# A new order for the last output projection, the router and the expert selection of an encoder layer

## The chip, the cores and the metric

One core of a Trainium2 chip runs one launch of the kernel. The metric is the device time of that launch in microseconds (us). The kernel before takes 1476.27 us, the median of three runs (1474.61, 1476.27 and 1476.34).

## What is computed

One encoder layer on 512 tokens with 1024 features, all in float32. After attention, four tiles of 128 tokens go through an output projection, a norm with a residual, a second norm, and a router that picks 4 of 32 experts for each token:

```python
mix = jnp.concatenate([o_diff, o_nat], axis=-1) @ w_out[l]
x = x + gt1 * rms_norm(mix, g_post_mix[l])
h2 = rms_norm(x, g_pre_ffn[l]) * (1.0 + sc2) + sh2
logits = (h2 @ w_router + b_router)          # 512 x 32
top_val, top_idx = lax.top_k(logits, TOP_K)  # 4 of 32
gates = softmax(top_val)
# each expert: y = swiglu_clamped(rows @ w1[e] + b1[e]) @ w2[e] + b2[e]
f = sum of gates * y over the chosen experts
x = x + gt2 * rms_norm(f, g_post_ffn[l])
```

Each expert's weights are 12 MB in float32, so the 32 experts bring 384 MB through the DMA engines.

## The kernel before

**Stages.** The kernel first does the modulation, the input projection and the two attentions. Then comes the stage in which the change lies, written out by hand for four token tiles (0 to 3), and after it 32 expert units, each of which takes 12 weight pieces of 1 MB and multiplies them with the rows of its tokens. Unit 0 has two row tiles of 32 slots, unit 1 has three.

**The order is the program's.** The stage is inside `manual_schedule`, so each engine gets its instructions in the order in which the code is written. Engines run beside each other and wait for one another by semaphores, but nothing on one engine overtakes what stands ahead of it there.

**The helpers of the stage**, with their engines and lines:

- `project_out(t, n)`: half n of the output projection of tile t, 24 matmuls of 128x512 on PE (L271 to L273), reading the split weights `wh` and `wl` and the split operands `mh` and `ml`.
- `gated(t, n)`: a square with a sum on ACT (L1066) and, on DVE, the product of the projection with a gain (L1067); the latter waits for the former.
- `mix_norm(t)` and `norm(t)`: ten tiny DVE operations each (L99 to L107), an inverse square root. `beside(...)` deals out the steps of several such generators in turn.
- `residual_in(t)`: on DVE twice the residual (L1077) and the product that gives `u` (L1079), on ACT two squares (L1080).
- `router_turn(t)`: 8 transposes of `u` on PE (L1112) and two copies `hT` on ACT (L1113).
- `router(t, tag)`: the router's products on PE (L1120, 8 calls, 16 records in the trace), which need `hT`.
- `write_h2(t)`: scales `u` on ACT (L1097), adds the shift `s2` on POOL (L1098) and writes the tile to DRAM by a DMA that POOL issues (L1102). For tile 3 the arithmetic is on DVE instead (L1101, two operations).
- `route(t)`: four DVE operations that pick the top 4 from the logits (L1132 to L1139).
- `place(t)`: small products of the choices on PE (L1147), which count the tokens ahead of each, then a DVE operation on that count (L1149) and one that makes a one-hot table `oh0` (L1151).
- `first_rows(t)`: the rows of tile t for the two experts of units 0 and 1, gathered on PE by that table into the PSUM tile `x0` (L1158, 16 matmul records).

After `first_rows(3)`, DVE subtracts one from `first` (L1258), transposes `x0` into `xt0` (L1259), and unit 0 begins on PE with L1535. On POOL the product of the last gain `gf` (L1027) follows the DMA of tile 3.

**The weight ring.** The pieces go through 14 slots of 1 MB, 4 in `rawa` and 10 in `rawb`. `feed.load()` (L143) puts the DMA of the next piece on SP's queue. The four slots of `rawa` are filled while the output weights are used up. `rawb` lies where the output weights and their operands were: `right.close()` gives that space back once the last projection is through, and then

```python
        right.close()
        rings.append(ctx.enter_context(tc.tile_pool(name="rawb", bufs=RING_B, side="right", reuse_waits="tile")))
        for _ in range(RING_B - 2):
            feed.load()
```

asks for eight pieces and, at the end of the stage, two more. From then on each of the 12 steps of a unit frees a slot and asks for one piece.

Of the kernel before, what the change touches and what calls it, by code (L numbers as in the profile page):

```python
# [59 lines left out]
def encoder_layer(ctx: ExitStack, tc: tile.TileContext, x, c, w_ada, b_ada, g_pre_mix, g_post_mix,  # L60
# [33 lines left out]
    def rstd_steps(pool, st):  # L94

        ss = st[:, 0:1]
        w = pool.tile([P, 3], F32, name="rq")
        y, h, q = w[:, 0:1], w[:, 1:2], w[:, 2:3]
        nc.vector.tensor_add(ss, ss, st[:, 1:2])  # L99
        nc.vector.tensor_scalar(ss, ss, 1.0 / D, EPS, ALU.mult, ALU.add)  # L100
        yield
        nc.vector.tensor_scalar(y.bitcast(I32), ss.bitcast(I32), -0.5, 1597463007.0, ALU.mult, ALU.add)
        nc.vector.tensor_scalar(h, ss, -0.5, None, ALU.mult)
        yield
        for i in range(3):
            nc.vector.scalar_tensor_tensor(out=q, in0=y, scalar=h, in1=y, op0=ALU.mult, op1=ALU.mult)
            nc.vector.scalar_tensor_tensor(out=ss if i == 2 else y, in0=q, scalar=1.5, in1=y, op0=ALU.add, op1=ALU.mult)  # L107
            yield
# [150 lines left out]
    def project_out(t, n=None, ks=range(KT)):  # L259
        if n is None:  # L260
            for n in range(2):
                project_out(t, n)
            return
        ns = halves[n]
        if ks[0] == 0:
            mixes.setdefault(t, []).append(pp.tile([P, 512], F32, tag=("mm", "S", "O", "mm")[t], name="mix"))
        mix = mixes[t][n]
        for k in ks:
            wh, wl = wo[k // 2]
            mh, ml = ops[t, k // 4]  # L270
            nc.tensor.matmul(mix, mh[:, k % 4, :], wh[:, k % 2, ns], start=(k == 0), stop=False)  # L271
            nc.tensor.matmul(mix, ml[:, k % 4, :], wh[:, k % 2, ns], start=False, stop=False)
            nc.tensor.matmul(mix, mh[:, k % 4, :], wl[:, k % 2, ns], start=False, stop=(k == KT - 1))  # L273
# [727 lines left out]
    with ExitStack() as m:  # L1001
# [27 lines left out]
        def residual(t):  # L1029
            res[t] = mo.tile([P, D], F32, name="res", bufs=2)  # L1030
            nc.sync.dma_start(res[t], xr[t])
# [28 lines left out]
        def gated(t, n):  # L1060

            if n == 0:
                sts[t] = o2.tile([P, 4], F32, name="st", bufs=4)
                us[t] = o2.tile([P, D], F32, name="u", bufs=4)
            ns, mix = halves[n], mixes[t][n]
            nc.scalar.activation(us[t][:, ns], mix, AF.Square, accum_out=sts[t][:, n:n + 1])  # L1066
            nc.vector.tensor_tensor(out=x1[:, t, ns], in0=mix, in1=gp[:, ns], op=ALU.mult)  # L1067

        def mix_norm(t):
            return rstd_steps(o2, sts[t][:, 0:2])  # L1070

        def residual_in(t):

            st = sts[t]
            u = us[t]
            for n, ns in enumerate(halves):
                nc.vector.scalar_tensor_tensor(out=x1[:, t, ns], in0=x1[:, t, ns], scalar=st[:, 0:1], in1=res[t][:, ns],  # L1077
                                               op0=ALU.mult, op1=ALU.add)
                nc.vector.tensor_mul(u[:, ns], x1[:, t, ns], a2[:, ns])  # L1079
                nc.scalar.activation(res[t][:, ns], x1[:, t, ns], AF.Square, accum_out=st[:, 2 + n:3 + n])  # L1080

        def norm(t):
            return rstd_steps(o2, sts[t][:, 2:4])

        def beside(*steps):

            steps = list(steps)
            while steps:
                for s in list(steps):
                    if next(s, steps) is steps:  # L1090
                        steps.remove(s)

        def write_h2(t):

            u, r2 = us[t], sts[t][:, 2:3]
            if t < NT - 1:
                nc.scalar.activation(u, u, AF.Copy, scale=r2)  # L1097
                nc.gpsimd.tensor_tensor(out=u, in0=u, in1=s2, op=ALU.add)  # L1098
            else:
                for ns in halves:  # L1100
                    nc.vector.scalar_tensor_tensor(out=u[:, ns], in0=u[:, ns], scalar=r2, in1=s2[:, ns], op0=ALU.mult, op1=ALU.add)  # L1101
            nc.gpsimd.dma_start(rows_of[0][t * P:(t + 1) * P, :], u)  # L1102

        def router_turn(t):

            hTs[t] = []
            for q in range(2):
                tp = pp.tile([P, 4, P], F32, tag="T", name="tp")
                hT = o2.tile([P, 4, P], F32, name="hT", bufs=4)
                for j in range(4):  # L1110
                    k = q * 4 + j
                    nc.tensor.transpose(tp[:, j, :], us[t][:, k * P:(k + 1) * P], ident)  # L1112
                nc.scalar.activation(hT, tp, AF.Copy)  # L1113
                hTs[t].append(hT)

        def router(t, tag):

            lg = lgs[t] = pp.tile([P, 512], F32, tag=tag, name="lg")[:, :NE]
            for k in range(KT):
                nc.tensor.matmul(lg, hTs[t][k // 4][:, k % 4, :], wr[:, k, :], start=(k == 0), stop=(k == KT - 1))  # L1120
# [8 lines left out]
        def route(t):  # L1129

            lo = lo4[:, t, :NE]
            nc.vector.scalar_tensor_tensor(out=lo, in0=lgs.pop(t), scalar=sts[t][:, 2:3], in1=br, op0=ALU.mult, op1=ALU.add)  # L1132
            yield

            nc.vector.max(top8[:, t, :], lo4[:, t, :])
            yield
            nc.vector.match_replace(rest[:, t, :], top8[:, t, :], lo4[:, t, :], -3.0e38)
            yield
            nc.vector.tensor_tensor(out=packed[:, t, 0, :], in0=rest[:, t, :NE], in1=lo, op=ALU.is_lt)  # L1139
            yield  # L1140

        def place(t):


            ps = pp.tile([P, 4, P], F32, tag="T", name="ps")[:, 0, :STATIC]
            for u in range(t + 1):
                nc.tensor.matmul(ps, tri if u == t else allone, packed[:, u, 0, :STATIC], start=(u == 0), stop=(u == t))  # L1147
            at = first[:, t, :]
            nc.vector.scalar_tensor_tensor(out=at, in0=ps, scalar=1.0, in1=packed[:, t, 0, :STATIC], op0=ALU.add, op1=ALU.mult)  # L1149
            yield  # L1150
            nc.vector.tensor_scalar(oh0[:, t, :], slot1, at[:, 0:1], None, ALU.is_equal)  # L1151
            yield

        def first_rows(t):

            for q in range(2):
                for c in range(4):
                    nc.tensor.matmul(x0[c * T:(c + 1) * T, q * SMALL:(q + 1) * SMALL], oh0[:, t, q * T:(q + 1) * T],  # L1158
                                     us[t][:, c * SMALL:(c + 1) * SMALL], start=(t + q == 0), stop=(t == NT - 1),
                                     skip_group_check=True)  # L1160
# [58 lines left out]
        residual_in(1)  # L1219
        beside(norm(1))  # L1220
        residual(3)
        router(0, "S")
        project_out(3, 0)
        for n in range(2):
            gated(2, n)
        beside(mix_norm(2))
        router_turn(1)
        write_h2(1)
        residual_in(2)
        beside(norm(2), route(0))  # L1230
        gated(3, 0)
        project_out(3, 1)
        right.close()
        rings.append(ctx.enter_context(tc.tile_pool(name="rawb", bufs=RING_B, side="right", reuse_waits="tile")))
        for _ in range(RING_B - 2):
            feed.load()
        gated(3, 1)
        router(1, "S")
        router_turn(2)
        write_h2(2)  # L1240
        beside(mix_norm(3), place(0), route(1))
        x0 = pp.tile([P, 512], F32, tag="S", name="x0")
        first_rows(0)
        router(2, "O")
        residual_in(3)
        beside(place(1), route(2))
        router_turn(3)
        first_rows(1)
        beside(norm(3), place(2))
        router(3, "O")  # L1250
        first_rows(2)
        beside(route(3))
        write_h2(3)
        beside(place(3))
        first_rows(3)
# [9 lines left out]
    with ExitStack() as m:  # L1265
# [477 lines left out]
        with tc.If(n_over > 0):  # L1743
            with tc.For_i(0, n_over, 1) as v:
                place = nc.gpsimd.value_load(over_i[0:1, bass.ds(v, 1)], min_val=0, max_val=NE - 1)
# [76 lines left out]
```

## Time and profile before

| what | value |
|---|---|
| median of three runs | 1476.27 us (1474.61 to 1476.34) |
| profiled execution, its own time | 1475.74 us |
| its span on the core | 1474.2 us |
| mean granted TensorE clock | 0.934 of full |
| PE busy (matmul) | 1285.8 us, 87% of the span |
| DVE, ACT and POOL busy | 577.6, 275.1 and 309.9 us |
| moved by DMA | 487.38 MB, mean 331 GB/s |

The page gives busy time by engine, the span in 40 slices, DMA queues and the costliest groups of instructions. Times in the timeline count from the start of the span. A busy PE is modelled, since matmuls overlap; the clock column says which share of full speed the engine was granted: 1.00 is 2.4 GHz, 0.50 is 1.2 GHz.

### The profile page before, as it was taken

The numbers are of one execution on the slowest core, as the hardware profiler recorded it, in microseconds if no ns is written. First come the engines' busy times: TensorE is split into PE (matmuls) and PEld (weight loads), VectorE is DVE, ScalarE is ACT, GpSimd is POOL, SyncE is SP. The second block draws the span as 40 slices with busy tenths as digits, with TensorE's granted clock in tenths as the row PEclk, the third lists the DMA queues.
The fourth block names the chain that finished last, engine by engine and source line by source line (L and its number), as shares of the span: only waits on it lengthen the run. The fifth ranks groups of instructions, "written<-read, shape, count | busy, mean of one in ns | idle before, by whom it ended". The sixth has DMA issues, their size and how long they took to land. (4 is left out here: it accounts for less than half of the span.)

```text
span 1474.2 us, 41218 instructions
## 1 busy us (share of the span) xinstructions
PE 1285.8 (87%) x18034; PEld 796.7 (54%) x18034; DVE 577.6 (39%) x1527; ACT 275.1 (19%) x680; POOL 309.9 (21%) x337
## 2 busy tenths in 40 slices
PE   6999899789889979777779999998999998989562
PEld 4876777677445535433346555554656553545221
DVE  4778664657543323222232333332333322223114
ACT  3355343533201100001000110010101101011011
POOL 5103121223112211112120112223212221211103
PEclk7999999889699999999999999999999997979765
DMA  8746344364999999999999699999999999999992
GB/s 272 248 157 237 129 158 142 99 221 146 396 351 403 400 397 406 400 405 401 400 400 383 211 383 398 398 400 398 409 398 397 400 395 396 403 393 407 395 401 90
DMA packets 144009, 487.38 MB, mean 331 GB/s; under 512 B 15448, under 2 KB 44508, under 8 KB 127440
## 3 DMA queue, kind: packets, MB, share of 16 engines
q1 hardware_dynamic: 125136, 457.30, 79.8%
q0 software_dynamic: 18624, 27.39, 7.3%
q8 instruction: 142, 2.33, 0.6%
q14 instruction: 43, 0.35, 0.1%
q10 hardware_dynamic: 64, 0.02, 0.0%
HBM read 471.86 MB, written 21.09 MB: 334 GB/s over the span
## 5 line engine op out<-in xcount | busy, mean ns | idle before, releaser
L1535 PE MATMUL acc<-raw,xT 128*32 128x256 f32 x9984 | 574.7, 385 | 76.3 <-DMA raw<-in_w_dram 71.1
L1535 PEld LDWEIGHTS acc<-raw,xT 128*32 128x32 f32 x9984 | 316.7, 111 | 319.0 <-DMA raw<-in_w_dram 106.8
L1535 PE MATMUL acc<-raw,gT 128*32 128x256 f32 x5120 | 311.3, 395 | 33.9 <-DMA raw<-in_w_dram 32.1
L1476 DVE TENSOR_TENSOR acc<-acc,xt 128x512 f32<-128x512 f32 (+1 forms) x140 | 83.5, 601 | 618.7 <-PE acc L1535 608.3
L1535 PEld LDWEIGHTS acc<-raw,gT 128*32 128x32 f32 x5120 | 165.1, 113 | 163.0 <-DMA raw<-in_w_dram 38.9
L1504 POOL DMA_INDIRECT f_d<-y,ri x79 | 125.3, 1586 | 495.4 <-issue 174.1
L1456 POOL DMA_INDIRECT gx<-h_d,ri x78 | 81.3, 1043 | 329.7 <-DVE gt L1451 245.4
L1486 ACT ACTIVATE g<-acc 128x256 f32<-128x256 f32 (+1 forms) x96 | 33.4, 348 | 535.8 <-DVE acc L1476 535.8
L1500 ACT ACTIVATE y<-acc,gt 128x256 f32<-128x256 f32 x79 | 33.0, 471 | 208.8 <-DVE acc L1476 157.5
L1493 DVE STREAM_TRANSPOSE gT<-g 128x256 f32<-128x256 f32 (+1 forms) x96 | 55.8, 581 | 3.3
L1487 DVE TENSOR_SCALAR lin<-acc 128x256 f32<-128x256 f32 (+1 forms) x96 | 36.5, 380 | 41.6 <-ACT g L1486 41.6
L728 ACT ACTIVATE s<-s,mx 128x512 f32<-128x512 f32 (+2 forms) x64 | 40.6, 636 | 50.7 <-DVE mx L726 50.7
L1465 DVE STREAM_TRANSPOSE xT<-gx 128x512 f32<-128x512 f32 (+3 forms) x33 | 41.6, 1260 | 3.6 <-DMA gx<-h_d,ri 3.6
L305 PE MATMUL ps<-hTh,wh 128*128 128x512 f32 x96 | 40.0, 416 | 1.2 <-ACT wh L334 1.2
L306 PE MATMUL ps<-hTh,wl 128*128 128x512 f32 x96 | 38.3, 399 | 1.2 <-DVE wl L340 1.2
L307 PE MATMUL ps<-hTl,wh 128*128 128x512 f32 x96 | 38.3, 399 | 0.0
L1523 ACT ACTIVATE xt<-ps 128x512 f32<-128x512 f32 (+1 forms) x62 | 27.0, 489 | 58.6 <-PE ps L1522 58.6
L1488 DVE SCALAR_TENSOR_TENSOR g<-g,lin 128x256 f32<-128x256 f32 (+1 forms) x96 | 36.6, 381 | 3.3
L726 DVE CUSTOM_DVE_ANT_0 s<-S,tab 128x512 f32<-128x512 f32 (+2 forms) x64 | 35.1, 586 | 7.0 <-PE S L757 6.9
L834 POOL TENSOR_TENSOR tab<-mask,rb 128x256 f32<-128x256 f32 (+1 forms) x24 | 21.9, 937 | 53.9 <-DVE mx L726 33.4
L1522 PE MATMUL ps<-bias,sl 128*128 128x256 f32 (+1 forms) x128 | 32.7, 379 | 0.0
L1522 PEld LDWEIGHTS ps<-bias,sl 128*128 128x128 f32 x128 | 22.8, 199 | 17.5 <-issue 14.0
(388 smaller groups left out, 1399.9 us busy)
## 6 DMA issues: line engine op xcount, KB each, us to landing
raw<-in_w_dram SPq DMA_DIRECT2D x384, 1024.0 KB
raw<-in_w_ada_dram SPq DMA_DIRECT2D x24, 1024.0 KB
raw<-in_w_in_dram SPq DMA_DIRECT2D x9, 1024.0 KB
rpb_q<-rpb_d SPq DMA_DIRECT2D x8, 512.0 KB
raw<-in_w_out_dram SPq DMA_DIRECT2D x4, 1024.0 KB
raw<-in_w_in_dram SPq DMA_DIRECT2D x12, 256.0 KB
xin<-in_x_dram SPq DMA_DIRECT2D x8, 256.0 KB
rb<-rpb_q POOLq DMA_DIRECT2D x8, 256.0 KB, 2.9
```

Source lines behind the costliest of these rows:

```text
L305: nc.tensor.matmul(ps, ah, bh, start=(k == 0), stop=False)
L306: nc.tensor.matmul(ps, al, bh, start=False, stop=False)
L307: nc.tensor.matmul(ps, ah, bl, start=False, stop=(k == n - 1))
L728: nc.scalar.activation(s, s, AF.Exp, bias=mx, scale=-1.0, accum_out=sums)
L1456: nc.gpsimd.indirect_dma_start(self.gx[:, t * SMALL:(t + 1) * SMALL], None, h2_d, self.quarter_rows(t), bounds_check=4 * L - 1, oob_is_err ...
L1465: nc.vector.transpose(xT[:, :self.n], self.gx[:, :self.n * SMALL].rearrange("p (t i k) -> p t k i", i=T, k=KT))
L1476: nc.vector.tensor_tensor(out=acc, in0=acc, in1=v, op=ALU.add)
L1488: nc.vector.scalar_tensor_tensor(out=g, in0=g, scalar=LIMIT_GLU, in1=lin, op0=ALU.min, op1=ALU.mult)
L1493: nc.vector.transpose(self.gT[:, half, ts[0]:ts[-1] + 1], g.rearrange("p (t i b) -> p t b i", i=T, b=4))
L1504: nc.gpsimd.indirect_dma_start(f_d, self.quarter_rows(t), self.y[:, t], None, bounds_check=4 * L - 1, oob_is_err=False, compute_op=ALU.add)
L1522: nc.tensor.matmul(ps, self.sl, bias[:, part, o:o + n], start=(part == 0), stop=(part == 1))
L1535: nc.tensor.matmul(acc[(c0 + c) * T:(c0 + c + 1) * T, :], b.stationary(third, k, t), w[:, c * SMALL:(c + 1) * SMALL], start=(k == 0 and t ...
```

## The change

`router(0)` and, of tile 1, `router_turn` and `write_h2` move from between the last projections to behind them. `route(0)`, `place` and `first_rows` of tiles 0 to 2 move later: `residual_in(3)` and `router_turn(3)` now come ahead of all `place` and `first_rows`, and `router(3)` ahead of all `first_rows` but the first. No operation is added or removed.

```diff
         residual(3)
-        router(0, "S")
         project_out(3, 0)
         for n in range(2):
             gated(2, n)
         beside(mix_norm(2))
-        router_turn(1)
-        write_h2(1)
         residual_in(2)
-        beside(norm(2), route(0))
+        beside(norm(2))
         gated(3, 0)
         project_out(3, 1)
         right.close()
         rings.append(ctx.enter_context(tc.tile_pool(name="rawb", bufs=RING_B, side="right", reuse_waits="tile")))
         for _ in range(RING_B - 2):
             feed.load()
+        router(0, "S")
+        router_turn(1)
+        write_h2(1)
         gated(3, 1)
         router(1, "S")
         router_turn(2)
         write_h2(2)
-        beside(mix_norm(3), place(0), route(1))
+        beside(mix_norm(3), route(0), route(1))
+        router(2, "O")
+        residual_in(3)
+        router_turn(3)
+        beside(norm(3), place(0), route(2))
         x0 = pp.tile([P, 512], F32, tag="S", name="x0")
         first_rows(0)
-        router(2, "O")
-        residual_in(3)
-        beside(place(1), route(2))
-        router_turn(3)
+        router(3, "O")
+        beside(place(1), route(3))
         first_rows(1)
-        beside(norm(3), place(2))
-        router(3, "O")
+        beside(place(2))
         first_rows(2)
-        beside(route(3))
         write_h2(3)
         beside(place(3))
         first_rows(3)
```

On PE, around the second last half of the projection (`wh`, `wl` are its weights, `mh`, `ml` its operands), the router's products go:

```order
 L272 MATMUL mix<-wh_3050,ml 128x512
 L273 MATMUL mix<-wl_3051,mh 128x512
-L1120 MATMUL lg<-wr,hT 128x32 x8
 L271 MATMUL mix<-wh_2882,mh 128x512
 L272 MATMUL mix<-wh_2882,ml 128x512
```

The same happens to the eight transposes of tile 1 between the last two halves, so 48 projection matmuls now follow each other on PE.

On ACT, from the squares of tile 2's projection on (`x_70` is the residual stream, `u` the tile before and after scaling):

```order
 L1066 ACTIVATE u,st<-mix 128x512 x2
+L1080 ACTIVATE res,st<-x_70 128x512 x2
+L1066 ACTIVATE u,st<-mix 128x512
 L1113 ACTIVATE hT<-tp 128x512 x2
 L1097 ACTIVATE u<-u,st 128x1024
-L1080 ACTIVATE res,st<-x_70 128x512 x2
-L1066 ACTIVATE u,st<-mix 128x512 x2
+L1066 ACTIVATE u,st<-mix 128x512
 L1113 ACTIVATE hT<-tp 128x512 x2
 L1097 ACTIVATE u<-u,st 128x1024
```

The copies and the scaling of tile 1 now stand behind the first and ahead of the second of the two squares of tile 3's projection.

On PE, the end of the stage before, from the transposes of tile 3 to unit 0 (the instructions of `place`, L1147, are left out here):

```order
L1112 MATMUL tp<-ident,u 128x128 x8
L1158 MATMUL x_3750<-u,oh_3449 32x256 x8
...
L1120 MATMUL lg<-wr,hT 128x32 x8
L1158 MATMUL x_3750<-u,oh_3449 32x256 x8
...
L1158 MATMUL x_3750<-u,oh_3449 32x256 x8
L1535 MATMUL acc<-raw,xt_3231 32x256 x16
```

and in the changed kernel:

```order
L1112 MATMUL tp<-ident,u 128x128 x8
L1147 LDWEIGHTS tri
L1147 MATMUL ps<-packed,tri 128x2
L1158 MATMUL x_3794<-u,oh_3449 32x256 x8
L1120 MATMUL lg<-wr,hT 128x32 x8
...
L1158 MATMUL x_3794<-u,oh_3449 32x256 x8
...
L1158 MATMUL x_3794<-u,oh_3449 32x256 x8
...
L1158 MATMUL x_3794<-u,oh_3449 32x256 x8
L1535 MATMUL acc<-raw,xt_3231 32x256 x16
```

Behind the transposes of tile 3 three `first_rows` stood before, of which one ahead of the last router products and two behind; now four stand there, three of them behind, each behind a `place`. The order on POOL and on SP is the same in both kernels.

## Rows read from the trace of the kernel before

**Rows 1.** The page, part 2: 40 slices of 36.9 us, busy tenths of DMA.

```profile
DMA  8746344364999999999999699999999999999992
```

**Rows 2.** SP's timeline: start, us, loads of 1 MB pieces.

```profile
360.41 1062.37 SPq L143 DMA_DIRECT2D raw<-in_w_dram  x380
...
387.51 0.37 SPq L143 DMA_DIRECT2D raw<-in_w_dram  x1
```

**Rows 3.** By stretch: PE, PEld, DVE, ACT, POOL busy, granted clock, DMA share, GB/s.

```profile
368.70:388.50 19.80, 16.39 (x114) 9.29 (x115) 11.88 (x38) 2.55 (x6) 3.44 (x6) 0.50 1.01 407
...
421.00:422.00 1.00, 1.00 (x14) 0.41 (x10) 0.00 (x0) 0.00 (x0) 0.70 (x2) 0.50 0.41 148
```

**Rows 4.** PE's timeline: start, us, instruction, in brackets idle time before and releaser.

```profile
346.61 1.86 PE L1120 MATMUL lg<-wr,hT 128*128 128x32 f32 x16
348.31 0.48 PE L271 MATMUL mix<-wh,mh 128*128 128x512 f32 x1
...
353.89 1.04 PE L1112 MATMUL tp<-ident,u 128*128 128x128 f32 x8
354.68 0.48 PE L271 MATMUL mix<-wh,mh 128*128 128x512 f32 x1
...
360.22 1.86 PE L1120 MATMUL lg<-wr,hT 128*128 128x32 f32 x16
```

**Rows 5.** ACT's timeline: tile 1's copies and scaling, later tile 3's second square.

```profile
354.52 1.09 ACT L1113 ACTIVATE hT<-tp 128x512 f32<-128x512 f32 x2 [3.90 <-PE tp L1112]
355.49 1.15 ACT L1097 ACTIVATE u<-u,st 128x1024 f32<-128x1024 f32 x1
356.54 0.63 ACT L1080 ACTIVATE res<-x 128x512 f32<-128x512 f32 x1
...
360.42 0.60 ACT L1066 ACTIVATE u<-mix 128x512 f32<-128x512 f32 x1 [1.97 <-PE mix L273]
```

**Rows 6.** POOL's timeline: shifts of tiles 1 and 2, a write's issue, the gain `gf`.

```profile
356.74 2.93 POOL L1098 TENSOR_TENSOR u<-u,s 128x1024 f32<-128x1024 f32 x1 [10.36 <-ACT u L1097]
...
364.86 2.35 POOL L1098 TENSOR_TENSOR u<-u,s 128x1024 f32<-128x1024 f32 x1 [4.33 <-ACT u L1097]
367.50 0.57 POOL L1102 DMA_DIRECT2D h_d<-u  x1 [0.30 <-POOL u L1098]
...
380.73 2.37 POOL L1027 TENSOR_TENSOR gf<-gf,gv 128x1024 f32<-128x1024 f32 x1
```

**Rows 7.** DVE's timeline: ten steps of a norm (first, last), and tile 3's path.

```profile
337.90 0.15 DVE L99 TENSOR_TENSOR st<-st 128x1 f32<-128x1 f32 x1
...
339.68 0.16 DVE L107 SCALAR_TENSOR_TENSOR st<-rq 128x1 f32<-128x1 f32 x1
...
364.92 2.30 DVE L106 SCALAR_TENSOR_TENSOR rq<-rq 128x1 f32<-128x1 f32 x1
...
367.90 0.75 DVE L1077 SCALAR_TENSOR_TENSOR x<-x,st,res 128x512 f32<-128x512 f32 x1
...
370.07 0.69 DVE L1079 TENSOR_TENSOR u<-x,a 128x512 f32<-128x512 f32 x1
...
380.30 2.94 DVE L1258 TENSOR_SCALAR first<-first 128x8 f32<-128x8 f32 x1
```

**Rows 8.** PE's timeline from the transposes of tile 3's second half to unit 0.

```profile
370.89 1.11 PE L1112 MATMUL tp<-ident,u 128*128 128x128 f32 x4 [0.28 <-DVE first L1149]
...
373.91 3.60 PE L1120 MATMUL lg<-wr,hT 128*128 128x32 f32 x16
377.44 1.94 PE L1158 MATMUL x<-u,oh 128*32 128x256 f32 x16
379.31 0.24 PE L1147 MATMUL ps<-packed,allone 128*128 128x2 bf16 x3
...
380.32 1.93 PE L1158 MATMUL x<-u,oh 128*32 128x256 f32 x16 [0.75 <-DVE oh L1151]
383.81 3.64 PE L1535 MATMUL acc<-raw,xt 128*32 128x256 f32 x32 [1.55 <-DVE xt L1259]
```

## The prediction, made before the changed kernel ran

> **What bounds the kernel now.** I began with the page's 40 slices [rows 1]: DMA is busy at nine tenths or more in 28 of the 29 slices from 369 us to the last but one, so the last three quarters of the span are the stream of expert weights. SP's timeline dates it [rows 2]: 380 loads of 1 MB from 360.41 on, 1062 us for 380 MB, with little left beside it. That makes an earlier first load look like pure gain. Two more rows speak against it. The eleventh new load goes out only at 387.51 [rows 2], because the 14 slots are full until unit 0, which begins at 383.81 [rows 8], has finished its first step of 3.64 us. And at 421 us DMA falls to 0.41 of its capacity while PE works without a pause [rows 3]: the loads have caught up and wait for slots. So until about 425 us the experts are paced by when unit 0 starts and by what PE does then, not by the stream. What moves unit 0's start moves the rest of the kernel by as much; what moves the first load alone is given back in that wait.
>
> The question is thus the path to 383.81. I read it backwards on PE [rows 8], then on DVE and POOL [rows 6, 7]: last product of tile 3 on DVE (start 370.07, 0.69 long, so ready at 370.76), transposes, router, rows of the last tiles, unit 0. It takes 13.05 us from 370.76, at a granted clock of 0.50 throughout [rows 3], 1.2 GHz.
>
> **What the change does to the first load.** The router's products of tile 0 (346.61 to 348.31, 1.70 us) and the transposes of tile 1 (353.89 to 354.68, 0.79 us) leave PE's way before the last projection [rows 4]. Its end moves from 360.22 to 357.73, and the loads, which wait for it, start 2.5 us earlier. By the argument above this is worth nothing unless unit 0 starts earlier too. SP's own order is unchanged, so no load is queued behind a new wait. The DMA that writes tile 1 goes out some 5 us later; nobody reads it before the gathers that follow unit 0's start, so I cost it at nothing.
>
> **What it does to tile 3's path.** Tile 1's work now lies behind the last projection, in the stretch where only tile 3 is waited for.
>
> - PE: 357.73 + 1.70 + 0.79 gives 360.22 for the end of the transposes of tile 1; they start at 359.43, and ACT's copies follow 0.63 us behind their start [rows 4, 5], at 360.06.
> - ACT: the copies hold it 0.97 us, the scaling 1.05 [rows 5]. Behind these now stands the second square of tile 3, at 360.06 + 2.02 = 362.08 where it was at 360.42 [rows 5]: 1.7 us later, although its projection is done 2.5 us earlier.
> - POOL: the shift of tile 1 starts 1.25 us after the scaling does [rows 5, 6], at 361.03 + 1.25 = 362.28, and lasts 2.35 us [rows 6] to 364.63. The issue of its write ends 0.86 us later (364.86 + 2.35 = 367.21 to 368.07 [rows 6]), so the shift of tile 2 runs from about 365.5 to 367.9.
> - DVE: the long rows show that a tiny operation on 128x1 takes 2.30 us where it meets such a shift, 364.92 to 367.22 against POOL's 364.86 to 367.21 [rows 6, 7]. Before, tile 3's norm met one of the two shifts, tile 2's. Now it meets both: it cannot start before 364.63, does 0.9 us of work until the shift of tile 2 begins, and goes on at 367.9. The ten steps of the norm take 1.94 us alone (337.90 to 339.84 [rows 7]); for the eight steps of two `route` between them I add 0.8, an estimate, for they fill waits between dependent steps. Of 2.74 us 0.9 are done, so it ends at 369.74. `residual_in(3)` takes 2.86 us (367.90 to 370.76 [rows 7]): ready at 372.6 instead of 370.76, **+1.8 us**.
>
> **What it does to the way from there to unit 0.** Before, the rows of tiles 0 and 1 were gathered ahead of the router of tile 3, one of them while PE had nothing better to do. Now all four gathers stand behind the transposes of tile 3, each behind a `place` that PE must wait for. At the low clock of the stretch, by rows 8:
>
> - 0.13 to the transposes (370.76 to 370.89) and 1.11 for them;
> - four gathers of 1.87 (377.44 to 379.31), 7.48;
> - the router's products 3.53 (373.91 to 377.44);
> - four times a `place` with its two DVE operations, 1.01 each (379.31 to 380.32), 4.04;
> - from the last gather's end (380.32 + 1.87 = 382.19) to unit 0 1.62, of which some 0.7 was lost before, since L1258 was held until POOL had finished `gf` (380.30 + 2.94 = 383.24 against 380.73 + 2.37 = 383.10 [rows 6, 7]). Now `write_h2(3)` sits on DVE during the third gather, and `gf` is through by then: 0.9.
>
> The sum is 17.2 us against 13.05, **+4.1 us**. Unit 0 starts at 372.6 + 17.2 = 389.8, **5.9 us** later than 383.81 (1.8 and 4.1).
>
> By then the earlier loads have been waiting with full slots: the ten are in by about 388.5 (2.5 us ahead of before), and the eleventh goes out at 389.8 + 3.7 = 393.5 instead of 387.51. So 5.9 us pass to the end in full. Against the profiled execution's own 1475.74 us that gives 1481.6; the median of the runs is 0.5 above that execution, so for the median **1482.2 us**. A measurement can tell about 0.2%, 3 us; the forecast is twice that.
>
> **Bounds of what the trace doesn't show.** The clock of the tail is at one end 0.50, as taken, at the other 1.00. I take 0.50: PE now stands still from about 365 (357.73, three routers, two tiles' transposes and short waits for copies) to 371, and in the stretch from 368.7 to 388.5 work of the same kind kept it busy for 16.39 of 19.80 us without bringing the clock back [rows 3]. The meeting of DVE with the shifts costs between nothing (3.6 us less than above: 1.2 of the first, 2.4 of the second) and what I took; I take the upper end, because the shift before did block DVE for its whole length [rows 6, 7]. A `place` costs at least the 0.24 of its PE rows and at most 1.01 [rows 8]; I take 1.01, as its three links are in series.
>
> **The rivals.**
>
> *The clock comes back before unit 0, or never leaves* (not slower). If PE ran at full speed over the tail, the PE pieces above, 1.11 + 7.48 + 3.53 = 12.1 us, would halve: 6.1 less. Unit 0's own slow start from 383.81 to 388.5 would also shrink by 2.35 [rows 3, 8]. 5.9 - 6.1 - 2.35 = -2.5: 1473.7. It decides at about 371: the clock must be 1.00 when the transposes of tile 3 run. For it: 7.5 us of unbroken work up to 365. Against it: the pause after it. Chance 0.06.
>
> *It comes back in the middle of the tail*, after the second gather: two gathers at half, 1.9, and the 2.35 of unit 0, 4.2 less: +1.7, 1478.0. PE is busier there than before. Against it: from 374 to 388.5 it was about as busy before and stayed at 0.50. Chance 0.12.
>
> *The shifts miss tile 3's norm*, because POOL comes later or DVE holds it off: 3.6 less, +2.3, 1478.6. For it: the order of two engines within tenths of a microsecond decides. Against it: either shift lies ahead of the norm's end by more than a microsecond. Chance 0.08.
>
> *`gf` holds the last one-hot.* In the new order `gf` on POOL starts about 0.1 us ahead of L1151 of tile 3 on DVE (an estimate: behind the start of the third gather L1151 comes by its 1.87 and half of a `place`, 2.37; `gf` by two operations of 0.69 like L1079 and the 0.30 and 0.57 of the write's issue, 2.25 [rows 6 to 8]). If L1151 waits as L1258 did [rows 7], the last gather starts some 2.2 us later: +8.1, 1484.4. The Trainium skill, "SBUF — State Buffer", Who interferes with whom, says that a VectorE operation with a single SBUF input also takes the port it shares with GpSimd when it is of the kinds that can run in a two-port mode, and names `tensor_scalar` among them, which L1151 is. The trace agrees for L1258, 2.94 us long; no run here yet shows L1151 beside a POOL operation that reads SBUF. Against it: 0.1 us decides. Chance 0.16.
>
> The forecast itself has 0.58.
>
> **How the numbers follow.** Slower by over 0.2%: the forecast and the last rival, 0.74. Within 0.2%: the middle return of the clock, the missed shifts, and a little of the first rival, 0.21. Faster by over 0.2% (below 1473.3): 0.05, out of the first rival's chance, should later slow stretches of unit 0 shrink as well. The range goes from 1478.0 less the 1.7 us by which the three runs differ, 1476.3, to 1484.4 and 1.7, 1486.1; it leaves out the first rival and the ends of the others.
>
> **What would show it.** The first load at about 357.9; the second square of tile 3 at about 362; two DVE operations of about 2 us between 362 and 368; PE idle from about 365 to 371; unit 0 at about 389.8; the granted clock at 0.50 in between; DMA nearly idle from about 388 to 394. The prediction is wrong if unit 0 starts before 386, or if DMA never pauses between 385 and 395, or if the end moves by another amount than unit 0's start.

## The result, and the profile after

The changed kernel takes 1485.15 us, the median of five runs (1482.04 to 1485.98), where the kernel before took 1474.61 on the same chip (five runs, 1473.64 to 1476.34). The ratio is 1.0058, with a 95% interval from 1.0042 to 1.0073: 8.6 us slower (6.2 to 10.8); the medians lie 10.5 us apart. The prediction was 5.9 us slower, with 0.74 for slower.

The times below count from the first `residual_in` of tile 1 on DVE (L1077), the point of reference. Before, unit 0 starts 37.22 us after it. This point lies ahead of everything that the change moves for tile 3, and it wanders from execution to execution: 346.59 us before, 348.56 in this profile, 345.27 in a second one of the changed kernel. Counted from the span's start, such wandering would look like an effect.

The 40 slices read as before [rows 1] but for two digits. The tenth slice rose from four to five tenths, since the loads start earlier; the eleventh, from 371 to 408 us, fell from nine to eight, for in it lies a pause.

```profile
DMA  8746344365899999999999699999999999999992
```

SP's timeline (start, us, loads of 1 MB pieces) answers to [rows 2]. The first load comes at 359.65, which is 11.09 us after the point of reference (13.82 before), the eleventh at 395.92, 47.36 us after the point of reference (387.51 before, 40.92 after it).

```profile
359.65 36.64 SPq L143 DMA_DIRECT2D raw<-in_w_dram  x11
...
395.92 0.37 SPq L143 DMA_DIRECT2D raw<-in_w_dram  x1
```

ACT, POOL and DVE show the path of tile 3 and the end of the stage [rows 5 to 7]: ACT's second square of tile 3, POOL's two shifts and `gf`, DVE's two held steps of the norm, the last `u` and the last one-hot.

```profile
363.84 0.60 ACT L1066 ACTIVATE u<-mix 128x512 f32<-128x512 f32 x1
```

```profile
364.04 2.35 POOL L1098 TENSOR_TENSOR u<-u,s 128x1024 f32<-128x1024 f32 x1 [15.69 <-ACT u L1097]
...
367.26 2.35 POOL L1098 TENSOR_TENSOR u<-u,s 128x1024 f32<-128x1024 f32 x1
...
386.83 2.35 POOL L1027 TENSOR_TENSOR gf<-gf,gv 128x1024 f32<-128x1024 f32 x1
```

```profile
365.17 1.23 DVE L99 TENSOR_TENSOR st<-st 128x1 f32<-128x1 f32 x1
...
367.40 2.24 DVE L107 SCALAR_TENSOR_TENSOR rq<-rq 128x1 f32<-128x1 f32 x1
...
373.03 0.69 DVE L1079 TENSOR_TENSOR u<-x,a 128x512 f32<-128x512 f32 x1
...
387.17 2.22 DVE L1151 TENSOR_SCALAR oh<-slot,first 128x128 f32<-128x128 bf16 x1
```

PE's timeline from the router of tile 2 to unit 0 answers to [rows 8]. PE now stands still for 4.84 us ahead of tile 3's transposes, and 2.50 us ahead of the last gather.

```profile
365.67 1.97 PE L1120 MATMUL lg<-wr,hT 128*128 128x32 f32 x16 [0.31 <-ACT hT L1113]
372.48 1.09 PE L1112 MATMUL tp<-ident,u 128*128 128x128 f32 x4 [4.84 <-DVE u L1079]
...
377.67 3.62 PE L1120 MATMUL lg<-wr,hT 128*128 128x32 f32 x16
...
389.44 1.94 PE L1158 MATMUL x<-u,oh 128*32 128x256 f32 x16 [2.50 <-DVE oh L1151]
392.22 3.64 PE L1535 MATMUL acc<-raw,xt 128*32 128x256 f32 x32 [0.84 <-DVE xt L1259]
```

By stretch (PE, PEld, DVE, ACT, POOL busy, granted clock, DMA share, GB/s; compare [rows 3]): the clock is 0.50 from tile 3's transposes through unit 0's first piece, and for three of these microseconds nothing is loaded.

```profile
372.50:392.20 19.70, 13.86 (x98) 8.09 (x98) 9.52 (x35) 1.83 (x4) 3.44 (x6) 0.50 0.99 408
392.20:397.60 5.40, 5.22 (x36) 2.69 (x37) 1.05 (x5) 0.50 (x2) 0.00 (x0) 0.50 0.12 17
...
393.00:396.00 3.00, 3.00 (x29) 1.20 (x22) 0.25 (x2) 0.00 (x0) 0.00 (x0) 0.50 0.00 0
```

So the last `u` starts at 24.47 (23.48 before), unit 0 at 43.66, **6.44 us** later than before. The shift stays: ACT's `g<-acc` operations in the expert units are 6.5 to 7.0 us late up to 630 us after the point of reference and 6.1 to 8.8 us behind that, and the last instruction on POOL (before, then changed) is 8.1 us late, 1128.62 against 1120.53.

```profile
1467.12 0.98 POOL L1722 DMA_INDIRECT out_dram<-gx,quarter  x1 [3.13 <-DMA out_dram<-raw,rows_out]
...
1477.18 0.98 POOL L1722 DMA_INDIRECT out_dram<-gx,quarter  x1 [3.14 <-DMA out_dram<-raw,rows_out]
```

### The profile page after: what moved, and what is told of

Read it like the earlier page. It is cut to its first block, busy times and chain, and to the rows that moved or that the text cites. A ratio compares the mean times of both kernels' runs of the same rounds, so it can differ in the third digit from the quotient of the medians.

```text
span 1484.2 us, 41215 instructions
## 1 busy us (share of the span) xinstructions
PE 1283.4 (86%) x18034; PEld 796.4 (54%) x18034; DVE 577.0 (39%) x1527; ACT 275.7 (19%) x680; POOL 309.5 (21%) x337
## 5 line engine op out<-in xcount | busy, mean ns | idle before, releaser
L306 PE MATMUL ps<-hTh,wl 128*128 128x512 f32 x96 | 38.2, 398 | 1.3 <-DVE wl L340 1.3
L81 DVE TENSOR_TENSOR ptl<-tp,pth 128x512 fp32r<-128x512 f32 (+2 forms) x48 | 25.2, 551 | 17.0 <-ACT pth L80 16.9
```

Source lines behind the costliest of these rows:

```text
L306: nc.tensor.matmul(ps, al, bh, start=False, stop=False)
```

## The experiments

The theory: unit 0's start sets the end; it is late because tile 3's norm meets two POOL shifts, because all gathers stand behind tile 3's transposes at half clock, and because `gf` holds the last one-hot; the earlier loads bring nothing. The rivals: the loads matter by themselves; VectorE's chain sets the tail whatever the clock; DVE is not really held by POOL. The last three columns are in us after the first residual of tile 1, each from one profiled execution. The ratio is to the kernel before on the same chip.

| kernel | median (runs) | ratio to before [95%] | first load | last `u` | unit 0 |
|---|---|---|---|---|---|
| before | 1474.61 (5) | 1 | 13.82 | 23.48 | 37.22 |
| changed | 1485.15 (5) | 1.0058 [1.0042, 1.0073] | 11.09 | 24.47 | 43.66 |
| e1_gain_on_dve | 1482.41 (6) | 1.0032 [1.0020, 1.0044] | 11.09 | 24.48 | 41.79 |
| e2_late_load | 1485.14 (5) | 1.0047 [1.0034, 1.0060] | 16.43 | 25.64 | 44.82 |
| e3_projection_only | 1482.79 (6) | 1.0035 [1.0022, 1.0048] | 11.08 | 24.78 | 40.24 |
| e4_tail_only | 1481.41 (9) | 1.0031 [1.0019, 1.0043] | 13.82 | 22.32 | 41.51 |
| after_again | 1486.75 (6) | 1.0053 [1.0035, 1.0071] | 11.09 | 24.47 | 43.65 |
| e5_warm_after | 1479.99 (12) | 1.0005 [0.9991, 1.0019] | 11.09 | 24.53 | 39.18 |
| e6_warm_before | 1475.65 (12) | 0.9978 [0.9966, 0.9990] | 13.82 | 23.50 | 34.24 |
| e7_no_shift | 1483.13 (12) | 1.0020 [1.0008, 1.0033] | 11.09 | 21.31 | 40.39 |
| e8_warm_gain_before | 1471.87 (12) | 0.9982 [0.9968, 0.9997] | 13.83 | 23.51 | 32.80 |
| e9_shift2_on_dve | 1470.85 (12) | 0.9975 [0.9960, 0.9990] | 13.83 | 21.41 | 31.18 |
| e10_warm_gain_after | 1470.72 (12) | 0.9978 [0.9963, 0.9994] | 11.09 | 24.55 | 36.41 |
| e11_early_loads | 1468.75 (12) | 0.9969 [0.9954, 0.9984] | 11.10 | 23.65 | 33.42 |

e1 to e4 ran on one chip (the kernel before 1477.87 there), after_again to e7 on a second (1479.16), e8 to e11 on a third (1474.24, and 1473.81 for e11). A ratio of one of these groups stands against one of another over different chips. The starts up to unit 0 don't suffer from that: in the two profiles of the changed kernel they agree within 0.01 us.

### Who holds the last one-hot: e1_gain_on_dve

```diff
         beside(norm(3), place(0), route(2))
+        gain(gf, 3)
...
-        gain(gf, 3)
```

Here `gain(gf, 3)` runs on DVE instead of POOL.

> The changed kernel with one difference: the product that finishes the gain gf goes from POOL at the stage's end to DVE, in the pause that DVE has while the router of tile 3 runs. As the lead-in to this stage differs by 1 to 2 us between executions, starts are counted from the first residual of tile 1 on DVE (346.59 before, 348.56 in the changed kernel): unit 0 stands 37.2 behind it before and 43.7 in the changed kernel. Theory A (unit 0's start sets the end, and 1.8 us of its delay is the last one-hot held by gf): the wait ahead of the fourth gather falls from 2.50 to about 0.7, unit 0 starts at 41.9, the end is 1.8 us earlier, about 1483.4. Theory B (the stream of weights sets the end, and the delay lies elsewhere): unit 0 at 41.9, the end unchanged at 1485.1.

Unit 0 came at 41.79, 1.87 sooner. DVE and PE show why (start, us, instruction): `gf` takes 1.23 us on DVE, L1151 0.33 instead of 2.22, and the last gather waits 0.62 instead of 2.50.

```profile
376.35 1.23 DVE L1027 TENSOR_TENSOR gf<-gf,gv 128x1024 f32<-128x1024 f32 x1
...
386.56 0.33 DVE L1151 TENSOR_SCALAR oh<-slot,first 128x128 f32<-128x128 bf16 x1
```

```profile
386.95 1.94 PE L1158 MATMUL x<-u,oh 128*32 128x256 f32 x16 [0.62 <-DVE oh L1151]
```

So 1.87 of the 6.44 us are `gf` on POOL. Whether the end followed, as Theory A has it, is not shown: the ratio of 1.0032 is below the changed kernel's 1.0058 and 1.0053, but these come from other chips, and the intervals overlap.

### What the earlier loads are worth: e2_late_load

```diff
-        for _ in range(RING_B - 2):
-            feed.load()
         router(0, "S")
...
         gated(3, 1)
+        late_d = drp.tile([P, 2], F32, name="late_d")
+        nc.sync.dma_start(late_d, sts[3][:, 0:2])
+        for _ in range(RING_B - 2):
+            feed.load()
```

> The changed kernel with its first expert loads held back: SP first issues a tiny DMA that needs the second square of tile 3, so the first load goes out about 5 us later (some 16.2 behind the first residual of tile 1, against 11.1). Theory A (until about 425 us the experts are paced by unit 0 and what PE does then; the DMA engines stand still for 5 us anyway, at 392 to 397): unit 0 stays at 43.7 behind that residual, the pause of DMA shrinks to nearly nothing, the end stays within 1 us of 1485.1. Theory B (the stream sets the end): the end moves by about 5 us to 1490.

The loads started 5.34 us later than in the changed kernel (16.43 against 11.09), and the ratio did not grow: 1.0047 [1.0034, 1.0060] against 1.0053 and 1.0058. The 5 us of Theory B would have made it about 1.009. Unit 0 moved by 1.16 for a side effect, the norm's first step, which waits for the small DMA that reads the same statistics:

```profile
366.70 1.06 DVE L99 TENSOR_TENSOR st<-st 128x1 f32<-128x1 f32 x1 [3.33 <-DMA late_d<-st]
```

So while unit 0 is this late, the start of the loads is worth nothing that can be measured, as argued.

### One half of the change at a time: e3_projection_only and e4_tail_only

e3 takes the kernel before and moves only tile 1's work and `router(0)` behind the projection; e4 takes the changed kernel and puts these back, so that only the tail is new.

```diff
-        router(0, "S")
         project_out(3, 0)
...
-        router_turn(1)
-        write_h2(1)
         residual_in(2)
-        beside(norm(2), route(0))
+        beside(norm(2))
...
             feed.load()
+        router(0, "S")
+        router_turn(1)
+        write_h2(1)
         gated(3, 1)
...
-        beside(mix_norm(3), place(0), route(1))
+        beside(mix_norm(3), route(0), route(1))
+        beside(place(0))
```

> The kernel before with the first part of the change alone: tile 1's transposes and write and tile 0's router products go behind the last projection, all that follows keeps its old order. Theory A: first load about 11.1 behind the first residual of tile 1 (before 13.8), the norm of tile 3 meets both shifts of POOL, its last product comes about 1 us later, unit 0 at 38.2 (before 37.2), end about 1 us later, 1475.6. Theory B (the first load counts): the end is 2.7 us earlier than before, 1472.

Unit 0 came at 40.24, not at 38.2: a miss. PE (e3) shows what was overlooked: `place(0)` now waits 5.09 us for the choice of `route(0)`, which comes late on DVE, and the gather and the router of tile 2 behind it run at half clock ahead of tile 3's transposes, for which `u` had been ready.

```profile
369.74 0.18 PE L1147 MATMUL ps<-packed,tri 128*128 128x2 bf16 x1 [5.09 <-DVE packed L1139]
370.70 1.94 PE L1158 MATMUL x<-u,oh 128*32 128x256 f32 x16 [0.78 <-DVE oh L1151]
372.57 3.62 PE L1120 MATMUL lg<-wr,hT 128*128 128x32 f32 x16
...
379.86 1.95 PE L1120 MATMUL lg<-wr,hT 128*128 128x32 f32 x16
```

In e4, against the changed kernel:

```diff
+        router(0, "S")
         project_out(3, 0)
...
+        router_turn(1)
+        write_h2(1)
         residual_in(2)
-        beside(norm(2))
+        beside(norm(2), route(0))
...
-        router(0, "S")
-        router_turn(1)
-        write_h2(1)
         gated(3, 1)
...
-        beside(mix_norm(3), route(0), route(1))
+        beside(mix_norm(3), route(1))
```

> The changed kernel with tile 0's router products and tile 1's transposes and write put back where they were: only the new order of selections and gathers remains. Theory A: first load as before (13.8 behind the first residual of tile 1), the norm of tile 3 meets one shift, its last product as before, the way from there to unit 0 as in the changed kernel, 18.5 instead of 13.05: unit 0 at about 42.6, end about 5.4 us later than before, 1480. Theory B (the delay comes from tile 1's work behind the projection): unit 0 and the end as before, 1474.6.

Unit 0 came at 41.51, 4.29 later than before, where 5.4 were expected: the last `u` started 1.16 sooner than before, although the shift of tile 2 held L1079 (2.71 us instead of 0.69). Here `place(0)`, with its wait for PE, no longer stands between the steps of tile 3's norm, and the norm was through before that shift began.

```profile
367.17 2.71 DVE L1079 TENSOR_TENSOR u<-x,a 128x512 f32<-128x512 f32 x1
```

Each half alone makes the kernel slower, by 0.35% and 0.31%. They don't add up to the whole (3.0 and 4.3 against 6.44 at unit 0): in e3 the loss is `place(0)` and what follows it ahead of tile 3's transposes, an order that the changed kernel doesn't have.

### What the clock costs: after_again, e5_warm_after, e6_warm_before

Matmuls whose output nobody reads fill PE's pauses; operands and output tile are long free.

```diff
+        def warm(n):
+            d = pp.tile([P, 512], F32, tag="mm", name="warm")
+            for i in range(n):
+                nc.tensor.matmul(d, bias[:, 0, :P], bias[:, 1, :512], start=(i == 0), stop=(i == n - 1))
...
+        warm(20)
         router_turn(3)
...
+        warm(4)
         first_rows(0)
...
+        warm(3)
         first_rows(1)
...
+        warm(3)
         first_rows(2)
...
+        warm(10)
         first_rows(3)
```

This is e5; e6 has `warm` in the order of the kernel before, with 5, 8, 3 and 4 ahead of `first_rows(0)`, `router_turn(3)`, `first_rows(2)` and `first_rows(3)`.

> The changed kernel once more, beside the three below and in the same runs of the kernel before, as their yardstick. All theories: unit 0 starts 43.7 us after tile 1's first residual on DVE (+6.4 over the kernel before) and the end is 6 to 9 us later than the kernel before.

It came as expected: unit 0 at 43.65, 7.6 us slower by the medians.

> Adds matmuls of 128x512 whose output nobody reads: 20 ahead of tile 3's transposes (4.6 us of the 4.84 us pause), 4, 3, 3 and 10 ahead of the four gathers. Theory A (TensorE's pause is what drops the clock to 0.50, and the low clock is what makes the tail long): the granted clock stays near 1.00 to unit 0, router(3) takes 2.0 us instead of 3.6 and each gather 1.1 instead of 1.9, unit 0's first piece 2.0 instead of 3.6; unit 0 comes about 4 us sooner (39.5 us after tile 1's first residual instead of 43.7), and the end some 6 us sooner than the changed kernel's. Theory B (VectorE's chain of selections sets the tail whatever the clock): unit 0 moves by less than 1 us. Theory C (such matmuls don't keep the clock): the clock is 0.50 as before and the added matmuls make unit 0 later.

Theory A held. The clock stayed at 1.00 (by stretch, columns as above), the router of tile 3 took 1.97 us, unit 0's first piece 1.93:

```profile
372.00:384.00 12.00, 10.92 (x108) 6.58 (x106) 7.79 (x27) 0.22 (x1) 3.48 (x6) 1.00 1.01 421
```

```profile
364.45 4.82 PE L1158 MATMUL warm<-bias 128*128 128x512 f32 x20
...
373.50 1.97 PE L1120 MATMUL lg<-wr,hT 128*128 128x32 f32 x16
...
384.72 1.93 PE L1546 MATMUL acc<-raw,xt 128*32 128x256 f32 x32 [0.84 <-DVE xt L1270]
```

Unit 0 came 4.47 us sooner than in after_again, the end 6.8 us (medians); 1.7 us of the difference are unit 0's own first piece. `gf` still held L1151, now for 3.08 us.

> The kernel before with such matmuls in its pauses: 5 ahead of the first gather, 8 ahead of tile 3's transposes, 3 and 4 ahead of the third and fourth gather. Theory A: the clock stays near 1.00, router(3) and the gathers shrink to half, unit 0 starts about 33 us after tile 1's first residual instead of 37.2, and the end is 5 to 6 us sooner than the kernel before. Theory B: unit 0 within 1 us of 37.2, end the same. Theory C: later by 1 to 3 us.

Unit 0 came 2.98 us sooner than in the kernel before (4 expected) and the end 3.3 (0.22%), so the half clock was a loss in the kernel before too. It fell again ahead of unit 0, when `gf` held L1258 (L1268 in this kernel) and PE had only 1.71 us of work in 4:

```profile
379.58 2.93 DVE L1268 TENSOR_SCALAR first<-first 128x8 f32<-128x8 f32 x1
```

```profile
380.00:384.00 4.00, 1.71 (x32) 0.76 (x28) 4.00 (x7) 0.00 (x0) 2.90 (x5) 0.98 1.01 415
384.00:388.00 4.00, 3.59 (x27) 1.97 (x20) 0.11 (x1) 0.72 (x2) 0.00 (x0) 0.59 1.01 423
```

### What the two shifts cost: e7_no_shift

```diff
-                nc.gpsimd.tensor_tensor(out=u, in0=u, in1=s2, op=ALU.add)
+                if t == 0:
+                    nc.gpsimd.tensor_tensor(out=u, in0=u, in1=s2, op=ALU.add)
```

> The changed kernel without the addition of s2 on POOL for tiles 1 and 2 (their h2 rows then lack the shift). Theory A (the two additions hold tile 3's norm on DVE: 1.23 and 2.24 us for steps of about 0.2): those two steps take 0.2 to 0.3 us, the last u starts about 3 us sooner (21.5 us after tile 1's first residual instead of 24.5), unit 0 2 to 3 us sooner. Theory B (the steps behind the norm wait for ScalarE or TensorE anyway): the last u moves by less than 1 us. The wait for gf ahead of the last gather (2.5 us) stays in both.

This kernel leaves out the addition of `s2` for tiles 1 and 2. L99 took 0.15 and the first L107 0.16 us (DVE), the last `u` started 3.16 us sooner, at 21.31, and unit 0 came 3.26 us sooner than in after_again, the end 3.6 us (medians).

```profile
365.23 0.15 DVE L99 TENSOR_TENSOR st<-st 128x1 f32<-128x1 f32 x1
...
366.38 0.16 DVE L107 SCALAR_TENSOR_TENSOR rq<-rq 128x1 f32<-128x1 f32 x1
```

Of these 3.2 us some 2.1 were there before the change: the one shift that it meets there holds the norm for 2.30 us [rows 7].

### What can be had: e8, e9, e10 and e11

e8_warm_gain_before is e6 with `gf` on DVE:

```diff
-                (nc.gpsimd if m == 3 else nc.vector).tensor_tensor(out=dst, in0=dst, in1=gains[m], op=ALU.mult)
+                nc.vector.tensor_tensor(out=dst, in0=dst, in1=gains[m], op=ALU.mult)
```

> The kernel before with the same added matmuls as e6_warm_before and gain(gf, 3) on DVE behind the last transpose instead of POOL. Theory A (POOL's 2.35 us on gf is all that held L1268, 2.93 us in e6_warm_before, and that stop dropped the clock ahead of unit 0): this step takes 0.2 to 0.3 us, unit 0 starts 31.6 us after tile 1's first residual (34.2 in e6_warm_before, 37.2 before) at a clock of 1.00, and the end is 3 to 4 us sooner than e6_warm_before, some 7 us sooner than the kernel before. Theory B (the units behind it wait for loads in any case): unit 0 sooner, the end as in e6_warm_before.

The clock stayed at 1.00. Unit 0 came at 32.80, 1.44 sooner than in e6 and 1.2 later than expected, since part of the hold had run beside the last gather. But the ratio of 0.9982 is not better than e6's 0.9978 (on another chip).

e9, against e8:

```diff
-            if t < NT - 1:
+            if t < NT - 2:
                 nc.scalar.activation(u, u, AF.Copy, scale=r2)
...
-        write_h2(2)
         beside(mix_norm(3), place(0), route(1))
...
-        warm(8)
         router_turn(3)
         first_rows(1)
+        write_h2(2)
         beside(norm(3), place(2))
```

> As e8_warm_gain_before, without the 8 matmuls ahead of tile 3's transposes, and tile 2's scaling and shift in one step on DVE (as tile 3's, 2 x 0.7 us) ahead of norm(3), instead of ACT and POOL. Theory A (tile 2's shift on POOL holds tile 3's mix norm by 2.1 us in the kernel before): no step of that norm takes over 0.3 us, the last u starts about 21.4 us after tile 1's first residual (23.5 before), and unit 0 comes 1 to 2 us sooner than in e8_warm_gain_before, since 1.4 us of DVE work moves into the tail. Theory B (DVE's chain in the tail takes all of it back): unit 0 within 0.5 us of e8_warm_gain_before.

The held step was gone, the last `u` started at 21.41 and unit 0 at 31.18, as Theory A said. The end did not follow: 0.9975.

e10 is e5 with the edit of e1 and without `warm(10)`.

> The changed kernel with the added matmuls of e5_warm_after (but the last ten) and gain(gf, 3) on DVE as in e1_gain_on_dve. Theory A (the clock and the wait for gf are separate losses and add up): L1151 takes 0.3 us, unit 0 starts 36.6 us after tile 1's first residual (39.2 in e5_warm_after, 41.8 in e1_gain_on_dve, 43.7 with the change alone), the end 2 to 3 us sooner than e5_warm_after, about 2 us sooner than the kernel before. Theory B (they overlap): unit 0 at 38 or later.

Unit 0 came at 36.41 (36.6 expected): the losses by the clock and by `gf` add up, and the changed order without them beats the kernel before by 0.22%. Unit 0 came 5.2 us later than in e9, but the loads started 2.74 us sooner, and the ends can't be told apart. The loads suggest why: in e8 DMA runs through without the pause that it made from 420 to 440 us before the change (0.94 of its capacity there), while in e10 there is still a short one from 410 to 420.

```profile
420.00:440.00 20.00, 20.00 (x380) 12.02 (x374) 6.16 (x13) 1.21 (x4) 1.58 (x1) 1.00 1.03 398
```

```profile
410.00:420.00 10.00, 5.96 (x93) 3.14 (x89) 4.45 (x30) 0.18 (x1) 2.99 (x3) 0.83 0.94 365
```

In the profiles of e8 and e9 the kernel is 9.2 and 9.4 us ahead of the kernel before (profiled on another chip) 110 us after the point of reference, and 5.5 and 5.8 ahead 76 us later; in e10 it is 5.6 and 4.8. So the lead that came from unit 0 was in part lost again. That speaks for the loads as the bound there, and then their start must count.

e11 is e9 with the moves of e3's first three pieces, and

```diff
+            if t < 1:
                 nc.scalar.activation(u, u, AF.Copy, scale=r2)
...
         write_h2(1)
+        beside(route(0))
         gated(3, 1)
...
+        router(2, "O")
         beside(mix_norm(3), place(0), route(1))
...
-        router(2, "O")
+        warm(4)
```

> As e9_shift2_on_dve (unit 0 31.2 us after tile 1's first residual, first load 13.8), with the part of the change that brings the loads forward: router(0), the transposes of tile 1 and its h2 behind the last projection, where tile 1's scaling and shift run on DVE too; router(2) goes ahead of the first gather. The first load comes at 11.1, unit 0 at 31 to 32. Theory A (once unit 0 no longer comes late, the stream of loads sets the end, so its start counts): the end is about 2.7 us sooner than that of e9_shift2_on_dve, a ratio of about 0.996 to the kernel before. Theory B (the first load is worth nothing, as argued for the change): 0.9975 as there.

The first load came at 11.10, unit 0 at 33.42 (31 to 32 expected), and in its profile the last instruction on POOL is 7.4 us ahead of the kernel before, against 4.7 in e9: 2.7 us more, as Theory A said. From the first load to that instruction it takes 1102.0 us in e8, 1102.1 in e9 and e11, and 1105.6 in e10 with its pause. But these are single profiles, and on the way e11 is between 2.0 us behind and 4.5 us ahead of e9. The ratio, 0.9969 [0.9954, 0.9984], is the lowest of all, but overlaps with e9's, so the runs don't tell the two theories apart, and that an earlier start of the loads counts here is not shown. e11 is faster than both kernels.

## Why the prediction was right, step by step

- *The earlier first load is worth nothing.* Right: 2.7 us earlier, and e2 shows no loss when they are taken away. It was tested only while unit 0 is late; where it is not, the profiles of e9 and e11 lie 2.7 us apart at the end, but their ratios don't show it.
- *Tile 3's norm meets both shifts, +1.8.* The mechanism was right (the square 1.45 us later, two DVE steps of 1.23 and 2.24 us), the size was not: +0.99. The step that failed is the work that I put behind the second shift, 1.84 us of the 2.74 with the 0.8 for the steps of `route`: five steps of the norm were done ahead of the hold, and the rest took 1.2 us. That shift also ended 0.26 us sooner than I had taken.
- *From the last `u` to unit 0, +4.1.* It was +5.45 (43.66 - 24.47 - 0.69 = 18.50 against 13.05). 1.87 of that is L1151 behind `gf`, by e1, which the term left out; without it 3.6. What is missing to the term is `place`: the four waits for it on PE come to 3.45 us (0.83, 0.83, 0.90 and, without `gf`, 0.89), where I had taken 1.01 each.
- *`gf` holds the last one-hot.* This rival, to which I gave 0.16, came true: `gf` started 0.34 us ahead of L1151, where I had estimated 0.1 and thought that either could come first. L1151 took 2.22 us, where 2.2 was the rival's price. The rule of the Trainium skill, "SBUF — State Buffer", Who interferes with whom, that a `tensor_scalar` can contend with GpSimd is borne out by this row, and by e1, where L1151 takes 0.33.
- *The clock stays at 0.50.* Right, from tile 3's transposes to 397.6 us.
- *The delay passes to the end in full.* Unit 0 +6.44, the end 8.1 in the profile and 8.6 [6.2, 10.8] by the ratio. Up to 630 us after the point of reference the profile shows it whole, 6.5 to 7.0 us. Whether the 2 us that came on top are real stays open: the interval reaches down to 6.2, and the shift between the two profiles wanders between 6.1 and 8.8 us behind that.

So the sum of 5.9 came near 6.44 by luck, by errors of opposite sign, and the case that occurred was that of the rival: 8.1 us at unit 0 there (1.8, 4.1 and 2.2), 6.44 measured (0.99, 3.6 and 1.87). That the median of 1485.15 lies so near the rival's 1484.4 is partly luck as well.

How much of the 6.44 is the order, and how much the clock and `gf`, can be read from e8 and e10, since both keep the clock at 1.00 to unit 0 and have `gf` on DVE: unit 0 at 32.80 in the old order and at 36.41 in the new. So about 3.6 us are the order itself, 1.0 of them ahead of the last `u` (23.51 and 24.55) and 2.6 behind it, where the gathers wait for each `place` in turn. The clock and `gf` together cost 4.4 us before and 7.3 after, 2.8 more.

## What to carry to other kernels

Follow what the moved work makes other engines wait for: here nothing was added, and some 3.6 us of the loss at unit 0 are work that now stands in series on the path to it, some 2.8 a longer tail at half of TensorE's clock and an operation on POOL that stops a small one of VectorE. Filling PE's pauses ahead of and in the serial tail, even with useless matmuls, was worth 6.8 us here, and an operation that nobody waits for soon belongs where it stops nobody. An earlier transfer brought nothing while the consumer that frees its slots was late itself; look which of the two binds after each edit.

## What the runs showed of the hardware

- Work on PE did not bring the clock back at once: over 5.22 us of work in 5.40 at unit 0's start it stayed 0.50, and in the kernel before from 370.89 to 379.6 us with no pause on PE; in e3 it came back while the tail still ran (a router of 3.62 us, and the next one 1.95). What makes the difference stays open. In e5, where the pauses were filled, it never left 1.00 on the way to unit 0.
- `gf` takes 2.35 us on POOL and 1.23 on DVE, and in every profile with it on POOL one DVE operation that takes 0.2 to 0.3 us alone took 2.2 to 3.1: L1258 [rows 7], or L1151.
